# Order on TensorE between layers: where the transposes of normed token tiles stand among the products

## The chip, the cores and the metric

The kernel runs on one core of a Trainium2 chip, in one launch. The metric is device time in microseconds. Before the change it is 3289.97 us (median of 3 runs, 3287.52 to 3290.29).

## What is computed

One sequence of 1024 tokens of width 1024 (float32) goes through two blocks of layers. Cut to what matters here, the reference is:

```
x = layernorm(a * x + rglru_mla(x))          # layer A: gated linear recurrence beside causal attention
x = layernorm(a * x + ssd(x))                # SSD layer: chunked state space scan
x = x + 0.5 * rms(swiglu(rms(x, pre1)), post1)   # first feed-forward layer, 2816 hidden
x = x + rms(mix(rms(x, pre_mix)), post_mix)      # mix layer: dilated attention beside an S5 scan
x = x + 0.5 * rms(swiglu(rms(x, pre2)), post2)   # second feed-forward layer
```

Each layer ends with a product of [1024 tokens x its width] by its output weights, a residual add and norms over each token's 1024 channels. The next layer begins with products that contract over the channels.

## The kernel before

**Layout.** Inside a layer the activations are feature-major (channels on partitions, tokens in the free dimension). A layer's last product is made by token tile: 8 tiles of 128 tokens. `out_tile` (L695) makes one tile, 128 tokens x 1024 channels, as two halves of 512 columns. Every operand of a product is split in a high and a low part (`split`, L140 on ScalarE and L141 on VectorE or POOL), and each product is three products of these. Layer A's and the SSD layer's out tiles take 36 matmuls, those of the feed-forward and the mix layer 24.

**A layer's end.** For each token tile i: products (TensorE), add to the residual (VectorE: L1123 in the SSD layer), norm (VectorE statistics, ScalarE, VectorE or POOL for gain and bias, L675 to L681; then ScalarE squares L1138 and the scaling L1148 where the next layer has a norm of its own), a store, and then TensorE transposes that make the tile feature-major: 8 of 128x128 in `transpose_tokens` (L212, for the SSD layer and the mix layer), or 16 for a pair of tiles in `Ops.build` (L1194, for the feed-forward layers, whose products are made by a seven-product scheme on blocks, so that ScalarE, VectorE and POOL also form sums of the transposed blocks before they split them). Build j takes tiles 2j and 2j + 1.

**The next layer's start.** `lead` (L202) makes the first two products of the SSD and the mix layer, each in a half for tokens 0 to 511 (tiles 0 to 3) and one for 512 to 1023 (tiles 4 to 7): first both first halves, then both second ones, 24 matmuls each. In `ffn`, the first slice of the hidden layer is made by `hidden(0, 256)` and `hidden(256, 512)` (L1287), 84 matmuls of 256 columns each (each build fills 128 of 512 columns: the first half needs builds 0 and 1, the second builds 2 and 3); later slices take 512 columns at once.

**What sets the order.** The program is traced instruction by instruction, and then a list scheduler sets the order within each engine by its own estimate. `issue_after(i)` holds what is traced in it behind instruction i in that order (no wait, only the order). `anchor(K)` (L99) is the TensorE instruction traced last, and `turn` (L168) traces something behind it. Before the change, out tiles and transposes aren't held: the scheduler puts them where it finds room, and out tiles 0 and 1 fill gaps in the last attention head. `K.last` is the last out tile's last instruction, behind which the next layer's first products stand.

**Buffers.** Out tiles use two PSUM buffers (psA), transposes four (psB). The normed tiles of a pair lie in one buffer of a pool of four (P2); in the SSD layer's end weights hold two of these, so that tiles 4 and 5 can only be loaded when build 0 has read tiles 0 and 1.

Of the kernel before, what the change touches and what calls it, by code (L numbers as in the profile page):

```python
# [18 lines left out]
P = 128  # L19
# [3 lines left out]
NK = D // P  # L23
# [27 lines left out]
def _pools(ctx, tc):  # L51
    K = Ctx()
# [20 lines left out]
    K.n = 0  # L73
    K.last = None

# [117 lines left out]
def lead(K, ws, xt):  # L193


    out = [K.A() for _ in ws]
    with K.tc.issue_after(anchor(K) if K.last is None else K.last):
        for h in (0, 512):
            for a, w in zip(out, ws):
                for k in range(NK):  # L200
                    for m, (l, r) in enumerate(((w[0], "h"), (w[0], "l"), (w[1], "h"))):
                        K.nc.tensor.matmul(a[:, h:h + 512], l[:, k, :], xt(r, k)[:, h:h + 512],  # L202
                                           start=k == 0 and m == 0, stop=k == NK - 1 and m == 2)
    return out
# [547 lines left out]
def layer_a_out(K, I, ydram, zd, x1, XT):  # L752
# [4 lines left out]
    an = [K.heads[-1]] * 2  # L757
# [4 lines left out]
    for i in range(NT):  # L762
        with deferred(K, an[i]):
            if i % 2 == 0:
                yl = K.L(F32R)
            yv = stream_rows(K, ydram, 2, i, yl[:, 512 * (i % 2):512 * (i % 2) + 512], n=2)
            yv += stream_rows(K, ydram, 4, i, tail=K.tail)
            z2 = K.P2()
            z, zl = z2[:, 0, :], z2[:, 1, :]
            nc.sync.dma_start(zl, zd[i * P:(i + 1) * P, :])  # L770
        a = K.A()
        out_tile(K, a, w, lambda k: yv[k], 6)
        an.append(anchor(K))
        nc.vector.tensor_tensor(z, zl, a, ALU.add)
        layernorm(K, z, g, b)
        nc.sync.dma_start(x1[i * P:(i + 1) * P, :], z)
        transpose_tokens(K, z, i, XT)
    K.last = an[-1]

# [263 lines left out]
class SsdOut:  # L1043
# [53 lines left out]
    def rest(self, flip):  # L1097
# [14 lines left out]
        for i in range(NT):  # L1112
# [4 lines left out]
            with deferred(K, an[i]):  # L1117
                yv = dict(zip((10, 11), stream_rows(K, self.yd, 10, i, self.half(i), n=2)))
                yv.update(zip(range(12, 16), stream_rows(K, self.yd, 12, i)))
                nc.sync.dma_start(z, self.zd[i * P:(i + 1) * P, :])  # L1120
            out_tile(K, a, [w[k] for k in order], lambda k: yv[order[k]], 6, 3, flip if i == 0 else None)
            an.append(anchor(K))
# [4 lines left out]
            if i % 2:  # L1127
                ops.build(zt[:, 0, :], z, i // 2)
            K.m.append(marks(K))
        K.last = an[-1]  # L1130
        K.m = K.m[3::4]
# [93 lines left out]
def ffn(K, w_in, w_out, ops, xin, gain, post_g, done, extra=None):  # L1225
# [84 lines left out]
    for t in range(N_HID):  # L1310
        with behind(K, K.m[t]) if t < 2 else nullcontext():
            w = weights(t)
        pt = K.P2()
        if t == 0:
            with K.tc.issue_after(anchor(K) if K.last is None else K.last):
                hidden(w, pt, 0, 256)
                an = anchor(K)
                hidden(w, pt, 256, 512)
        else:
            hidden(w, pt, 0, 512)  # L1320
        nc.sync.dma_start(hd[t], pt[:, 0, :])
        tick(3)
# [125 lines left out]
    for i in range(NT):  # L1448
# [4 lines left out]
        o = (i % 2) * 512 + (i // 2) * P  # L1453
        out_tile(K, a, w, lambda k: (hid[k][:, 0, o:o + P], hid[k][:, 1, o:o + P]), 4)
        an.append(anchor(K))
        K.last = an[-1]
        y = acc[i // 2][:, i % 2, :]
# [330 lines left out]
def mix_out(K, I, ydram, zd, x3, x4, ops):  # L1788
# [8 lines left out]
    for i in range(NT):  # L1797
# [10 lines left out]
        a = K.A()  # L1808
        out_tile(K, a, w, lambda k: yv[k], 4)
        an.append(anchor(K))  # L1810
        nc.vector.tensor_tensor(z, z, a, ALU.add)
        post_norm(K, z, x, post, 1.0, junk, i < 6)
        nc.sync.dma_start(x4[tk, :], x)
        pre_norm(K, x, z)
        if i % 2:
            ops.build(zt[:, 0, :], z, i // 2)
        K.m.append(marks(K))
    K.last = an[-1]
    K.m = K.m[3::4]
# [105 lines left out]
def tile_two_blocks(ctx, tc, I, out):  # L1925
# [16 lines left out]
    def done(i, x, y):  # L1942
        nc.sync.dma_start(x3[i * P:(i + 1) * P, :], x)
        pre_norm(K, x, y)
        transpose_tokens(K, y, i, XT)

# [34 lines left out]
```

## Time and profile before

| | |
|---|---|
| time, median of 3 runs | 3289.97 us (3287.52 to 3290.29) |
| profiled execution | 3289.96 us, span 3288.2 us |
| mean granted clock of TensorE | 0.969 |
| TensorE busy | 3082.6 us (94%) |
| VectorE, ScalarE, POOL busy | 2210.6, 1625.5, 779.2 us (67%, 49%, 24%) |
| DMA | 398.97 MB, 121 GB/s on average |

The busy time of TensorE is the sum over its matmuls as the profile has them; the rest of the span it stands still. The clock is a share of full speed. The layer ends lie at about 400 to 545 us (layer A), 1290 to 1414 us (SSD layer), 2060 to 2140 us (first feed-forward layer) and 2500 to 2640 us (mix layer) of the span.

### The profile page before, as it was taken

The numbers are of one execution on the slowest core, as the hardware profiler recorded it, in microseconds if no ns is written. First come the engines' busy times: TensorE is split into PE (matmuls) and PEld (weight loads), VectorE is DVE, ScalarE is ACT, GpSimd is POOL, SyncE is SP. The second block draws the span as 40 slices with busy tenths as digits, with TensorE's granted clock in tenths as the row PEclk, the third lists the DMA queues.
The fourth block names the chain that finished last, engine by engine and source line by source line (L and its number), as shares of the span: only waits on it lengthen the run. The fifth ranks groups of instructions, "written<-read, shape, count | busy, mean of one in ns | idle before, by whom it ended". The sixth has DMA issues, their size and how long they took to land. (4 is left out here: it accounts for less than half of the span.)

```text
span 3288.2 us, 42188 instructions
## 1 busy us (share of the span) xinstructions
PE 3082.6 (94%) x15560; PEld 2572.9 (78%) x15560; DVE 2210.6 (67%) x3637; ACT 1625.5 (49%) x2945; POOL 779.2 (24%) x487
## 2 busy tenths in 40 slices
PE   8999899999999899689999899899999799999898
PEld 6887777888898778578778777688787688888777
DVE  6537777365748555887775789636666955455997
ACT  5526544355545522655555443642565755554442
POOL 0000001123322221622233434100000432332543
PEclk9999999999999999899999999999999899999999
DMA  4157442335344555323332620354564322224223
GB/s 129 55 181 234 121 132 87 87 82 125 87 116 97 173 162 162 99 97 116 103 126 81 224 83 30 131 178 175 151 165 139 136 84 90 77 84 150 107 84 116
DMA packets 349566, 398.97 MB, mean 121 GB/s; under 512 B 21168, under 2 KB 279344, under 8 KB 349360
## 3 DMA queue, kind: packets, MB, share of 16 engines
q1 hardware_dynamic: 324016, 379.50, 36.7%
q10 hardware_dynamic: 25344, 16.78, 1.6%
q8 instruction: 123, 2.02, 0.3%
q14 instruction: 83, 0.68, 0.1%
HBM read 279.29 MB, written 116.92 MB: 120 GB/s over the span
## 5 line engine op out<-in xcount | busy, mean ns | idle before, releaser
L141 DVE TENSOR_TENSOR wlo<-wst,whi 128x1024 fp32r<-128x1024 f32 (+1 forms) x190 | 234.1, 1235 | 355.2 <-ACT whi L140 337.2
L185 PE MATMUL pa<-x,whi 128*128 128x512 f32 x1568 | 428.6, 394 | 1.8 <-DVE l L141 0.9
L140 ACT ACTIVATE whi<-wst 128x1024 fp32r<-128x1024 f32 (+1 forms) x190 | 179.9, 948 | 350.9 <-PE pa L185 85.7
L147 ACT ACTIVATE wst<-wst,pk 128x128 f32<-128x128 f32 (+1 forms) x816 | 251.7, 391 | 181.8 <-DMA wst<-in_ffn_w_in_dram 116.0
L185 PEld LDWEIGHTS pa<-x,whi 128*128 128x128 f32 x1568 | 291.5, 188 | 63.9 <-DVE x L141 1.7
L185 PE MATMUL pa<-x,wlo 128*128 128x512 f32 x784 | 244.0, 392 | 2.0 <-DVE wlo L141 2.0
L1287 PE MATMUL pb<-x,whi 128*128 128x512 f32 (+1 forms) x736 | 224.2, 381 | 0.3 <-DVE r L141 0.3
L1287 PE MATMUL pa<-x,whi 128*128 128x512 f32 (+1 forms) x736 | 220.5, 382 | 1.0 <-DVE lnt L280 0.5
L1366 PE MATMUL pa<-wlo,whi 128*128 128x512 f32 x768 | 191.1, 407 | 16.7 <-DVE wlo L141 15.1
L1366 PEld LDWEIGHTS pa<-wlo,whi 128*128 128x128 f32 x768 | 151.0, 198 | 54.4 <-DVE wlo L141 19.9
L1366 PE MATMUL pb<-wlo,whi 128*128 128x512 f32 x744 | 178.8, 398 | 14.4 <-DVE wlo L141 14.4
L1250 POOL TENSOR_TENSOR s<-wst 128x512 f32<-128x512 f32 x44 | 57.7, 1311 | 562.1 <-ACT wst L147 524.3
L1366 PEld LDWEIGHTS pb<-wlo,whi 128*128 128x128 f32 x744 | 141.9, 192 | 47.3 <-DVE wlo L141 17.7
L185 PEld LDWEIGHTS pa<-x,wlo 128*128 128x128 f32 x784 | 147.2, 188 | 36.1 <-DVE wlo L141 4.5
L937 POOL TENSOR_TENSOR s<-s,p 128x1024 f32<-128x1024 f32 x32 | 64.5, 2016 | 448.1 <-DMA s<-d 337.5
L1287 PEld LDWEIGHTS pa<-x,whi 128*128 128x128 f32 x736 | 135.8, 189 | 28.5 <-ACT p L1290 1.6
L1287 PEld LDWEIGHTS pb<-x,whi 128*128 128x128 f32 x736 | 136.1, 188 | 26.9 <-DVE r L141 0.5
L140 ACT ACTIVATE whi<-s 128x1024 fp32r<-128x1024 f32 x88 | 93.0, 1057 | 112.6 <-POOL s L1251 59.9
L891 PE MATMUL pa<-whi,x 128*128 128x256 f32 x512 | 147.9, 289 | 0.0
L892 PE MATMUL pa<-wlo,x 128*128 128x256 f32 x512 | 145.0, 283 | 1.9 <-DVE wlo L141 1.9
L893 PE MATMUL pa<-whi,x 128*128 128x256 f32 x512 | 144.9, 283 | 0.0
L681 POOL TENSOR_TENSOR p<-p,q 128x1024 f32<-128x1024 f32 x8 | 21.1, 2643 | 513.7 <-DVE p L680 476.8
(580 smaller groups left out, 8067.8 us busy)
## 6 DMA issues: line engine op xcount, KB each, us to landing
wst<-in_ffn_w_in_dram SPq DMA_DIRECT2D x88, 512.0 KB, 3.8
d<-p SPq DMA_DIRECT2D x82, 512.0 KB, 3.5
d<-l SPq DMA_DIRECT2D x67, 512.0 KB, 3.9
x<-d SPq DMA_DIRECT2D x128, 256.0 KB, 5.4
p<-d SPq DMA_DIRECT2D x46, 512.0 KB, 4.6
wst<-in_s_w_in_dram SPq DMA_DIRECT2D x40, 512.0 KB, 4.1
s<-d SPq DMA_DIRECT2D x32, 512.0 KB, 9.5
l<-d SPq DMA_DIRECT2D x24, 512.0 KB, 6.0
```

The source lines that it names most:

```text
L140: K.nc.scalar.activation(hi, src, AF.Copy)
L141: (eng or K.nc.vector).tensor_tensor(lo, src, hi.bitcast(F32), ALU.subtract)
L147: K.nc.scalar.activation(st[:, k, :], st[:, k, :], AF.Copy, scale=col(K, gain, k0 + k))
L185: K.nc.tensor.matmul(ps[:, h:h + 512], w, x[:, h:h + 512], start=k == 0 and m == 0, stop=k == n - 1 and m == 2)
L681: nc.gpsimd.tensor_tensor(z, z, b, ALU.add)
L891: nc.tensor.matmul(o, xh, wh, start=k == 0, stop=False)
L892: nc.tensor.matmul(o, xh, wl, start=False, stop=False)
L893: nc.tensor.matmul(o, xl, wh, start=False, stop=k == NK - 1)
L937: nc.gpsimd.tensor_tensor(mv, mv, per_head(csT, P), ALU.subtract)
L1250: G(s1, a21, a22, ALU.add)
L1287: nc.tensor.matmul(p, l[:, k, :], r[:, k, :], start=k + m == 0, stop=k == 3 and m == 2)
L1366: nc.tensor.matmul(bank[j], th[:, a + o:a + o + P], tw[:, b:b + 512], start=c + m == 0, stop=c == n - 1 and m == 2)
```

## The change

All out tiles are now traced in `turn`, so that they run one after the other as traced. The transposes are no longer traced where their tile is normed: they are put on a list, `K.late`, and traced later, each behind the TensorE instruction traced last.

- Layer A: tile i - 2's transposes behind tile i's products; tiles 6 and 7 within `lead`, tile 6 behind the first product's first half, tile 7 behind the second's.
- SSD layer: build j in the middle (behind 18 of 36 matmuls) of out tile 2j + 3; build 3, of tiles 6 and 7, directly behind out tile 7, before any product of the feed-forward layer.
- First feed-forward layer: tile i - 3 behind tile i; tile 5 behind the first product's first half in `lead`, tiles 6 and 7 ahead of the second halves.
- Mix layer: build j behind out tile 2j + 3; build 3 between `hidden(0, 256)` and `hidden(256, 512)`.

The number of matmuls and of all other instructions is the same.

```
 def lead(K, ws, xt):
     out = [K.A() for _ in ws]
-    with K.tc.issue_after(anchor(K) if K.last is None else K.last):
-        for h in (0, 512):
-            for a, w in zip(out, ws):
-                ...
+    late, K.late = K.late, []
+    def product(a, w, h):
+        ...
+    keep = 3 if len(late) > 2 else 2
+    for h in (0, 512):
+        for a, w in zip(out, ws):
+            while late and (h or len(late) > keep):
+                turn(K, late.pop(0))
+            turn(K, lambda: product(a, w, h))
+            keep -= 1

 layer_a_out, per tile i
-        out_tile(K, a, w, lambda k: yv[k], 6)
+        turn(K, lambda: out_tile(K, a, w, lambda k: yv[k], 6))
         ...
-        transpose_tokens(K, z, i, XT)
-    K.last = an[-1]
+        K.late.append(lambda z=z, i=i: transpose_tokens(K, z, i, XT))
+        if i > 1:
+            turn(K, K.late.pop(0))
+    K.last = anchor(K)

 SsdOut.rest, per tile i
-            out_tile(K, a, [w[k] for k in order], lambda k: yv[order[k]], 6, 3, flip if i == 0 else None)
+            mid = flip if i == 0 else K.late.pop(0) if i > 2 and i % 2 else None
+            turn(K, lambda: out_tile(K, a, [w[k] for k in order], lambda k: yv[order[k]], 6, 3, mid))
             ...
             if i % 2:
-                ops.build(zt[:, 0, :], z, i // 2)
+                K.late.append(lambda zt=zt, i=i: ops.build(zt[:, 0, :], zt[:, 1, :], i // 2))
+            if i == 7:
+                turn(K, K.late.pop(0))
-        K.last = an[-1]
+        K.last = anchor(K)

 ffn, first slice
-            with K.tc.issue_after(anchor(K) if K.last is None else K.last):
+            with K.tc.issue_after(K.last):
                 hidden(w, pt, 0, 256)
                 an = anchor(K)
-                hidden(w, pt, 256, 512)
+                while K.late:
+                    turn(K, K.late.pop(0))
+                turn(K, lambda: hidden(w, pt, 256, 512))

 ffn, per out tile
-        out_tile(K, a, w, lambda k: (hid[k][:, 0, o:o + P], hid[k][:, 1, o:o + P]), 4)
+        turn(K, lambda: out_tile(K, a, w, lambda k: (hid[k][:, 0, o:o + P], hid[k][:, 1, o:o + P]), 4))
         an.append(anchor(K))
-        K.last = an[-1]
+        if len(K.late) > 2:
+            turn(K, K.late.pop(0))
 (its caller's done: transpose_tokens goes on K.late)

 mix_out, per tile i
-        out_tile(K, a, w, lambda k: yv[k], 4)
+        turn(K, lambda: out_tile(K, a, w, lambda k: yv[k], 4))
         an.append(anchor(K))
+        if i > 2 and i % 2:
+            turn(K, K.late.pop(0))
         ...
-            ops.build(zt[:, 0, :], z, i // 2)
+            K.late.append(lambda zt=zt, i=i: ops.build(zt[:, 0, :], zt[:, 1, :], i // 2))
```

**What moves on TensorE, SSD layer's end, builds 0 and 1.** Line numbers grow by 8 to 13 (L695 becomes L703, L1194 L1207, L1287 L1300). Here pa_10501 is out tile 5 before and pa_10260 is out tile 3 after; the transposes of p_10232 are build 1's, those of p_10023 build 0's. A name's number tells buffers apart. Before, in tile 5:

```order
L695 MATMUL pa_10501<-wlo_10014,s_10505 128x512 x2
L1194 MATMUL pb_10385<-ident,p_10232 128x128 [waits PE_49,Activation_49]
L1194 MATMUL pb_10385<-ident,p_10232 128x128 x3
L1194 MATMUL pb_10390<-ident,p_10232 128x128 [waits DVE_49]
L1194 MATMUL pb_10390<-ident,p_10232 128x128 x3
L695 MATMUL pa_10501<-whi_10013,s_10505 128x512 x2
L1194 MATMUL pb_10395<-ident,p_10232 128x128 [waits PE_49,Activation_49]
```

After, in tile 3:

```order
L703 MATMUL pa_10260<-p_9996,s_10264 128x512
L1207 MATMUL pb_10297<-ident,p_10023 128x128 [waits Activation_49]
L1207 MATMUL pb_10297<-ident,p_10023 128x128 x3
L1207 MATMUL pb_10302<-ident,p_10023 128x128 x4
L1207 MATMUL pb_10307<-ident,p_10023 128x128 [waits Activation_49]
L1207 MATMUL pb_10307<-ident,p_10023 128x128 x3
L1207 MATMUL pb_10312<-ident,p_10023 128x128 x4
L703 MATMUL pa_10260<-p_10001,s_10264 128x512 x6
```

Before, tile 2's and 3's transposes stood apart, near the end of tile 5 (and tile 0's and 1's in tiles 3 and 4); after, the 16 of a pair stand together in the middle of an out tile, tile 0's and 1's in tile 3 and tile 2's and 3's in tile 5.

**The same layer's end, TensorE's order at the start of the feed-forward layer.** pa_10866 is a product of `hidden(0, 256)`, p_10424 and p_10616 are the normed tiles of builds 2 and 3 before. Before:

```order
L1287 MATMUL pa_10866<-q_10189,whi_10835 128x256
L1287 MATMUL pa_10866<-q_10190,whi_10835 128x256
L1287 MATMUL pa_10866<-q_10189,wlo_10836 128x256
L1194 MATMUL pb_10577<-ident,p_10424 128x128 [waits Activation_49]
L1194 MATMUL pb_10577<-ident,p_10424 128x128 x3
L1194 MATMUL pb_10582<-ident,p_10424 128x128 x4
L1194 MATMUL pb_10587<-ident,p_10424 128x128 [waits Activation_49]
L1194 MATMUL pb_10587<-ident,p_10424 128x128 x3
L1194 MATMUL pb_10592<-ident,p_10424 128x128 x4
L1194 MATMUL pb_10769<-ident,p_10616 128x128 [waits PE_49,Activation_49]
```

After (pa_10654 is out tile 7, p_10577 holds tiles 6 and 7, pa_10852 is the first product of `hidden(0, 256)`):

```order
L703 MATMUL pa_10654<-wlo_10014,s_10658 128x512 x2
L703 MATMUL pa_10654<-whi_10013,s_10658 128x512 x2
L1207 MATMUL pb_10769<-ident,p_10577 128x128 [waits PE_49,Activation_49]
L1207 MATMUL pb_10769<-ident,p_10577 128x128 x3
L1207 MATMUL pb_10774<-ident,p_10577 128x128 [waits DVE_49]
L1207 MATMUL pb_10774<-ident,p_10577 128x128 x3
L1207 MATMUL pb_10779<-ident,p_10577 128x128 [waits PE_49,Activation_49]
L1207 MATMUL pb_10779<-ident,p_10577 128x128 x3
L1207 MATMUL pb_10784<-ident,p_10577 128x128 [waits DVE_49]
L1207 MATMUL pb_10784<-ident,p_10577 128x128 x3
L1300 MATMUL pa_10852<-r_10291,whi_10835 128x256
```

Before, 36 matmuls of `hidden(0, 256)` stood between out tile 7 and the transposes of builds 2 and 3; after, build 3 stands directly behind out tile 7 and all 168 matmuls of the first slice behind build 3 (build 2 is in the middle of tile 7).

**TensorE at the end of layer A's attention.** pb_3346 is the last head's product, pa_3472 out tile 0, pa_3556 out tile 1. Before:

```order
L695 MATMUL pa_3472<-r_3450,s_3464 128x512
L695 MATMUL pa_3556<-r_3450,s_3548 128x512 x2
L400 MATMUL pb_3346<-p_1625,q_1510 128x256 [waits Activation_49]
L695 MATMUL pa_3472<-r_3450,s_3464 128x512 [waits DVE_49]
L695 MATMUL pa_3472<-r_3450,s_3464 128x512 x3
L695 MATMUL pa_3556<-r_3450,s_3548 128x512 x4
L400 MATMUL pb_3346<-p_1625,q_1510 128x256 [waits DVE_49]
```

After:

```order
L703 MATMUL pa_3472<-r_3450,s_3464 128x512
L408 MATMUL pb_3346<-p_1625,q_1510 128x256 [waits Activation_49]
L703 MATMUL pa_3472<-r_3450,s_3464 128x512 [waits DVE_49]
L703 MATMUL pa_3472<-r_3450,s_3464 128x512 x3
L408 MATMUL pb_3346<-p_1625,q_1510 128x256 [waits DVE_49]
```

Before, matmuls of out tiles 0 and 1 stood among the last heads' products, 30 of them tile 1's; after, only out tile 0's do, and all 36 of tile 1 stand behind tile 0's last.

## Rows read from the trace of the kernel before

**Rows 1.** The page, span and busy time of each engine.

```profile
span 3288.2 us, 42188 instructions
...
PE 3082.6 (94%) x15560; PEld 2572.9 (78%) x15560; DVE 2210.6 (67%) x3637; ACT 1625.5 (49%) x2945; POOL 779.2 (24%) x487
```

**Rows 2.** TensorE's waits, 1290 to 1400 us: total, times, longest.

```profile
PE pb L1194 <- ACT p L1148: 22.6, 5, 10.9
```

**Rows 3.** TensorE's timeline, 1294 to 1430 us: start, us, line, count, idle before.

```profile
1302.25 0.61 PE L695 MATMUL pa<-whi,l 128*128 128x512 f32 x2
...
1310.41 0.61 PE L695 MATMUL pa<-whi,l 128*128 128x512 f32 x2
...
1316.08 1.03 PE L1194 MATMUL pb<-ident,p 128*128 128x128 f32 x8
...
1345.54 1.97 PE L1194 MATMUL pb<-ident,p 128*128 128x128 f32 x8 [7.78 <-ACT p L1148]
1347.51 1.19 PE L695 MATMUL pa<-whi,l 128*128 128x512 f32 x2
...
1364.76 0.40 PE L1287 MATMUL pa<-r,whi 128*128 128x256 f32 x2
...
1384.72 1.97 PE L1194 MATMUL pb<-ident,p 128*128 128x128 f32 x8 [10.89 <-ACT p L1148]
...
1395.34 1.97 PE L1194 MATMUL pb<-ident,p 128*128 128x128 f32 x8 [2.54 <-ACT p L1148]
...
1413.52 0.70 PE L1287 MATMUL pa<-r,whi 128*128 128x512 f32 x2 [0.25 <-DVE p L1296]
```

**Rows 4.** ScalarE's timeline there: last activation of tiles 0, 1 and 7.

```profile
1313.55 1.15 ACT L1148 ACTIVATE p<-p,pns 128x1024 f32<-128x1024 f32 x1 [0.74 <-DVE pns L280]
...
1322.07 1.16 ACT L1148 ACTIVATE p<-p,pns 128x1024 f32<-128x1024 f32 x1
...
1394.14 1.15 ACT L1148 ACTIVATE p<-p,pns 128x1024 f32<-128x1024 f32 x1 [0.64 <-ACT x L140]
```

**Rows 5.** VectorE's timeline there: add of tiles 0 and 1.

```profile
1297.80 1.22 DVE L1123 TENSOR_TENSOR p<-p,pa 128x1024 f32<-128x1024 f32 x1
...
1303.43 1.22 DVE L1123 TENSOR_TENSOR p<-p,pa 128x1024 f32<-128x1024 f32 x1
```

**Rows 6.** POOL's timeline there: splits of build 0.

```profile
1334.58 2.54 POOL L141 TENSOR_TENSOR x<-p,x 128x512 fp32r<-128x512 f32 x2
...
1341.23 1.26 POOL L141 TENSOR_TENSOR q<-p,q 128x512 fp32r<-128x512 f32 x1
```

**Rows 7.** Windows: length, busy of PE, PEld, DVE, ACT, POOL, PEclk, DMA.

```profile
1340.00:1350.00 10.00, 4.46 (x15) 3.62 (x16) 7.26 (x15) 3.66 (x7) 2.49 (x2) 0.66 0.53 184
...
1380.00:1390.00 10.00, 3.94 (x16) 3.13 (x16) 8.16 (x28) 8.78 (x18) 2.35 (x1) 0.50 0.48 152
...
1400.00:1410.00 10.00, 10.00 (x84) 10.00 (x84) 7.12 (x16) 7.98 (x23) 1.27 (x2) 0.98 0.01 2
```

**Rows 8.** SP's queue there: loads of tiles 4 to 7.

```profile
1342.52 15.00 SPq L1120 DMA_DIRECT2D p<-d  x4
```

**Rows 9.** TensorE's waits, layer A's end (390 to 545 us).

```profile
PE pb L212 <- POOL p L681: 4.1, 1, 4.1
PE pa L695 <- ACT s L140: 3.8, 2, 3.2
```

**Rows 10.** Windows at the three other ends, columns as in rows 7.

```profile
530.00:540.00 10.00, 5.88 (x28) 4.41 (x27) 4.67 (x6) 3.40 (x5) 3.24 (x2) 0.84 0.26 107
...
2120.00:2130.00 10.00, 7.28 (x24) 5.90 (x25) 2.92 (x6) 6.79 (x15) 0.00 (x0) 0.53 0.00 0
...
2590.00:2600.00 10.00, 1.12 (x4) 0.72 (x4) 10.00 (x22) 10.00 (x27) 8.53 (x5) 0.58 0.31 127
```

**Rows 11.** TensorE's waits, first feed-forward layer's end (2060 to 2150 us).

```profile
PE pb L212 <- ACT p L1148: 8.0, 3, 5.1
```

**Rows 12.** TensorE's waits, mix layer's end (2540 to 2640 us).

```profile
PE pa L1287 <- ACT whi L140: 7.6, 1, 7.6
```

More of the change, by code (lines that the diff above doesn't have):

```diff
@@ L73, in _pools @@
     K.n = 0
-    K.last = None
+    K.last, K.late = None, []
     def nm(p):
@@ L196, in lead @@
     out = [K.A() for _ in ws]
-    with K.tc.issue_after(anchor(K) if K.last is None else K.last):
-        for h in (0, 512):
-            for a, w in zip(out, ws):
[L200 to L203, printed above, removed]
+    late, K.late = K.late, []
+    def product(a, w, h):
+        for k in range(NK):
+            for m, (l, r) in enumerate(((w[0], "h"), (w[0], "l"), (w[1], "h"))):
+                K.nc.tensor.matmul(a[:, h:h + 512], l[:, k, :], xt(r, k)[:, h:h + 512],
+                                   start=k == 0 and m == 0, stop=k == NK - 1 and m == 2)
+    keep = 3 if len(late) > 2 else 2
[5 more added lines that the diff above has]
+            keep -= 1
     return out
@@ L1815, in mix_out @@
         if i % 2:
-            ops.build(zt[:, 0, :], z, i // 2)
+            K.late.append(lambda zt=zt, i=i: ops.build(zt[:, 0, :], zt[:, 1, :], i // 2))
         K.m.append(marks(K))
-    K.last = an[-1]
+    K.last = anchor(K)
     K.m = K.m[3::4]
@@ L1944, in done @@
         pre_norm(K, x, y)
-        transpose_tokens(K, y, i, XT)
+        K.late.append(lambda: transpose_tokens(K, y, i, XT))
     ffn(K, I["ffn1_w_in"], I["ffn1_w_out"], ops, x2, "ffn1", I["ffn1_post_g"], done, s5_prep(K, I))
```

## The prediction

> **What bounds the kernel now.** The page comes first: its span, and TensorE's busy time. TensorE works 3082.6 of 3288.2 us [rows 1], so all that a new order can win is the 205 us in which it stands still, and whatever it makes TensorE wait is paid in full. The profiled execution took 3289.96 us, 1.8 us more than its span and 0.01 us from the median of the three runs, so the sum below is made against 3289.96. About 0.2%, 6.6 us, is what a measurement of this kernel can tell from no change.
>
> The change touches four places, where one layer's last eight token tiles are multiplied out, normed, transposed on TensorE and split for the next layer. I read the list of TensorE's waits there, then its timeline, then the other engines' at the same place. At the end of the SSD layer TensorE waits 22.6 us for the second norm's last activation, L1148 [rows 2]. The timeline shows where [rows 3]: transposes of tile 0 stand between products without a wait (1316.08, eight in 1.03 us), those of tile 3 come after 7.78 us of idleness (1345.54), those of tiles 4 to 7 start after 10.89 us more (1384.72) and end with tile 7's at 1395.34. Between the last out tile and that wait, 36 of the 84 products of the feed-forward layer's first half slice run (from 1364.76).
>
> **The SSD layer's end, the largest term.** The new order on TensorE is: tile 3's first 18 products, the 16 transposes of tiles 0 and 1, its other 18; the same in tile 5 for tiles 2 and 3, in tile 7 for tiles 4 and 5; then the transposes of tiles 6 and 7, and behind them all 168 products of the first slice. Nothing on TensorE may pass a transpose that waits. Removed is nothing, added nothing: all products and transposes stay, so the price is the idle time.
>
> A tile's 36 products take 8.16 us (1302.25 to 1310.41 [rows 3]), 0.227 us each. Between the end of tile 1 and the transposes that need it lie tile 2 and half of tile 3, 54 x 0.227 = 12.2 us. How long does a tile take from its last product to being normed? Tile 1's products end at 1302.25 and its last activation ends at 1322.07 + 1.16 = 1323.23 [rows 3, 4], 21.0 us. Tile 0 took 1313.55 + 1.15 - 1297.80 = 16.9 us from its add on VectorE [rows 4, 5], and the add of tile 1 came 1.2 us after its last product (1303.43 [rows 5]). 16.9 + 1.2 = 18.1: I take 18 us, with 16.9 (no lag at all) and 21.0 as ends. Tile 7 needed 1395.29 - 1364.76 = 30.5 us [rows 3, 4], with the next layer's weight work in the same queues; I don't take that, because its chain in the changed order has less in front of it, but it says on which side the error may lie. On POOL the new order puts each tile's norm behind the splits of the transposes just issued, and those are 1.3 us each [rows 6].
>
> 18 is more than 12.2, so each of the four groups of transposes waits. After such a wait the clock is at 1.2 GHz: 0.66 was granted over 1340 to 1350, 0.50 over 1380 to 1390 [rows 7], and eight transposes take 1.97 us, not 1.03 [rows 3]. So 16 take 3.9 us, and the 18 products behind them 4.1 + 1.2 = 5.3 us, since the first ones are still slow (two in 0.98 us at 1347.51 [rows 3], where two at 2.4 GHz take 0.45).
>
> By steps: the first group starts at 1323.2, tile 3 ends at 1323.2 + 3.9 + 5.3 = 1332.4; the second starts at 1332.4 + 18 = 1350.4, tile 5 ends at 1359.6, and tile 6 and half of tile 7 fit in the next 18 us. The third starts at 1377.6, tile 7 ends at 1386.8, and the fourth starts at 1404.8, with nothing of TensorE's beside the whole of tile 7's norm. At 1408.7 the first slice begins; its 168 products of 256 columns take 168 x 0.119 = 20.0 us (84 in 10 us over 1400 to 1410 [rows 7]). The second slice then starts near 1428.7, where before it started at 1413.5 [rows 3]: **+15 us**. In short the term is 3 x latency - 38.8. At 16.9 us it is +12, at 21.0 it is +24. Were TensorE at 2.4 GHz throughout (2.1 + 4.1 us a step in place of 9.2, 2.1 for the last group), it would lose another 11 us: at 16.9 us of latency that leaves **+1**. The ends are +1 and +24.
>
> The loads of tiles 4 to 7 wait on SP's queue for the first group's last split to free their buffer (four issues from 1342.52 [rows 8], just after POOL's split at 1341.23 [rows 6]). In the new order that group starts 7 us later than tile 0's transposes did, but all at once, so I let the loads come when they came; they are 5 us late at worst, within the ends. The waits give VectorE, ScalarE and POOL no more work. Who waits behind: hidden, and through it the whole first feed-forward layer.
>
> **Layer A's end.** TensorE waits 4.1 us for tile 7's transposes [rows 9], and the clock is slow around it (0.84 over 530 to 540, some 1.6 us [rows 10]). Before and after, 48 products of the SSD layer stand ahead of those transposes, so they gain only what tile 7's norm gains: the transposes of tiles 4 to 6 come sooner and their splits leave VectorE's queue ahead of it, 0 to 6 us. Given back: 30 products of out tile 1 filled the last attention head and now stand behind it, up to 30 x 0.227 = 6.8 us. But there was a wait of 3.2 us just there for a split (the larger part of 3.8 [rows 9]) which tile 1's products can now fill. I take 0, the ends are -6 and +7.
>
> The Trainium skill speaks against this part: "Perfetto Trace Analysis", section "Optimization Strategy", says that where the most contended engine changes over time, mixing the stages can help, and the change takes such mixing out. By that rule all 6.8 us would be lost and the sum would be 3309; the rows, with a wait beside it that the same products fill, leave it near 0.
>
> **First feed-forward layer's end.** Waits of 8.0 us for tiles 4, 6 and 7 [rows 11], the clock at 0.53 after them [rows 10]. The transposes of tile 5 move ahead of the second first-half product, by 5 us. Their splits leave ScalarE sooner, so tile 7's norm, queued behind them, can end some 2 us sooner: **-2**. At best it is 6 us (the wait of 5.1 in there, and some clock), at worst +4: tile 5 isn't normed where it is asked for, and 24 products stand behind it.
>
> **Mix layer's end.** VectorE is busy 10.00 of 10 us and TensorE 1.12 over 2590 to 2600 [rows 10], with 7.6 us of waiting for a weight split [rows 12]. The order of TensorE can't shorten VectorE's work; the last transposes now come after 84 products instead of among them. **-1**, from -6 (most of that wait) to +6 (the same again, for tile 7).
>
> **Sum**: 0 + 15 - 2 - 1 = +12, so 3289.96 + 12 = **3302 us**.
>
> **Rivals.**
> 1. Norms finish early. While TensorE waits, the others have less to do, and the latency is at the low end with little slow clock: +1 at the SSD layer, sum +1 - 3 = -2, 3288 us. For it: tile 0's 16.9 us [rows 4, 5]. Against it: POOL's splits in front [rows 6] and tile 7's 30.5 us. 0.18.
> 2. Faster. The transposes issued early take their splits out of ScalarE's and VectorE's queues before the last tile's norm, which then ends 5 us sooner at layer A's and the first feed-forward layer's end: -6 there, -6 there, and +2 at the SSD layer: -10, 3280 us. It decides if the latency at the SSD layer is below about 15 us (3 x 15 - 38.8 = +6, less the slow clock). For it: the waits of 4.1 and 8.0 us [rows 9, 11]. Against it: no tile in the trace was normed that soon. 0.14.
> 3. Mixing is lost (the page's rule above, as a mechanism of this kernel): the last head has only out tile 0 to fill with, and layer A costs +6.8: 3309 us. Against it: the wait of 3.2 us [rows 9]. 0.10.
> 4. The change does nothing that counts: the order was as good as this already at three places, and the waits at the fourth come out alike: 3290 us. Against it: the 36 products that stood before the last waits now stand behind them. 0.05.
>
> **How the numbers follow.** My forecast has 0.53 of the chance. Below 3283.4 lies rival 2 with a hair of rival 1: 0.15. Within 6.6 us of 3290 lie rivals 1 and 4 (0.18 + 0.05, less that hair): 0.22. The rest, the forecast and rival 3, is slower: 0.63. The forecast's own band is 3296 to 3314 (the SSD layer's term at +12 to +24, the others near their values). The range reaches down over rivals 1 and 4 and stops above rival 2, whose 0.14 it leaves out with the forecast's tail: 3284 to 3314.
>
> **What would show it.** Right: at the SSD layer's end four waits of transposes for L1148's counterpart in the new file, the last one the longest (some 15 us, before the feed-forward layer's first product), each followed by a clock near 0.5; the second slice starting 10 to 20 us later against the end of tile 1; the three other ends within 6 us of before. Wrong: a latency under 15 us in those rows, a first product of the feed-forward layer that comes as early as before, or a layer A whose attention loses more than 5 us of TensorE's time.

## The result and the profile after

The changed kernel takes **3318.35 us** (median of 4 runs, 3317.75 to 3320.36), beside 3289.18 us for the kernel before on the same chip (4 runs, 3287.52 to 3290.29): 29.2 us (0.9%) more by the medians, a ratio of 1.0096 with an interval of 1.0083 to 1.0108. The forecast was slower by 12 us, at most by 24.

The page first, against [rows 1]:

```profile
span 3316.2 us, 42147 instructions
...
PE 3078.8 (93%) x15560; PEld 2572.7 (78%) x15560; DVE 2225.8 (67%) x3637; ACT 1627.1 (49%) x2945; POOL 754.7 (23%) x487
```

TensorE's work is the same to 4 us, so the 28.0 us of span are time in which it stands still. TensorE's waits at the SSD layer's end (1280 to 1450 us), against the 22.6 us of [rows 2]; L1207 and L1161 are the transposes of a build and the norm's last activation, L1194 and L1148 before:

```profile
PE pb L1207 <- ACT p L1161: 46.4, 5, 15.5
```

TensorE's timeline there, against [rows 3]: all transposes of a build, and at other places the row in which a tile's or a slice's products begin or end.

```profile
1313.86 1.03 PE L1207 MATMUL pb<-ident,p 128*128 128x128 f32 x8
1322.00 1.97 PE L1207 MATMUL pb<-ident,p 128*128 128x128 f32 x8 [7.11 <-ACT p L1161]
...
1329.85 0.62 PE L703 MATMUL pa<-whi,l 128*128 128x512 f32 x2
...
1342.10 1.03 PE L1207 MATMUL pb<-ident,p 128*128 128x128 f32 x8
1352.48 1.97 PE L1207 MATMUL pb<-ident,p 128*128 128x128 f32 x8 [9.36 <-ACT p L1161]
...
1358.86 0.62 PE L703 MATMUL pa<-whi,l 128*128 128x512 f32 x2
...
1371.10 1.03 PE L1207 MATMUL pb<-ident,p 128*128 128x128 f32 x8
1386.02 1.97 PE L1207 MATMUL pb<-ident,p 128*128 128x128 f32 x8 [13.88 <-ACT p L1161]
...
1392.22 0.61 PE L703 MATMUL pa<-whi,s 128*128 128x512 f32 x2
1393.43 1.10 PE L1207 MATMUL pb<-ident,p 128*128 128x128 f32 x8 [0.59 <-ACT p L1161]
1410.02 1.97 PE L1207 MATMUL pb<-ident,p 128*128 128x128 f32 x8 [15.49 <-ACT p L1161]
1411.63 0.78 PE L1300 MATMUL pa<-r,whi 128*128 128x256 f32 x2
...
1433.37 0.70 PE L1300 MATMUL pa<-r,whi 128*128 128x512 f32 x2 [0.61 <-DVE p L1309]
```

Four long waits, each for the odd tile of a pair, and the longest ahead of the feed-forward layer's first product (1411.63). The second slice starts at 1433.37, 19.9 us later than in [rows 3]. Tile 1 ends 0.6 us sooner here, so this place costs 20.5 us.

To find the other 7.5 us I take the same points of the program in both traces and compare the stages between them. The points are the last product of a `lead`, the end of the SSD layer's out tile 1, the first out tile of a feed-forward layer, the first 512-column product of a first slice, the start of the last 48 products ahead of the second feed-forward layer's out tiles, and the last matmul. Differences from the profiled execution of before, in us (from one profiled execution each; columns 1, 3, 5 and 6 hold the four ends that the prediction lists):

| kernel | layer A and its end | to the SSD out tiles | SSD end | first ffn's slices | its end | mix layer and its end | second ffn, up to its out tiles | to the last matmul |
|---|---|---|---|---|---|---|---|---|
| after | 0.3 | -0.9 | **20.5** | -3.1 | -2.7 | **6.8** | **2.7** | **4.3** |
| e1 | 0.2 | 3.4 | 16.1 | -2.1 | -3.2 | 2.7 | 0.0 | 0.0 |
| e2 | -4.9 | -3.0 | 1.9 | -2.4 | -2.1 | 7.4 | 3.8 | 4.7 |
| e3 | -4.3 | -0.7 | 20.6 | -3.7 | -3.7 | -2.6 | -0.7 | 6.9 |
| e4 | 1.6 | 0.2 | 21.7 | -2.3 | -4.4 | 7.3 | 3.2 | 0.8 |
| e5 | 0.6 | -0.4 | 18.1 | -1.2 | -3.7 | 5.4 | 2.0 | 6.5 |
| e6 | -2.8 | -0.7 | 20.1 | -3.5 | -4.5 | 9.2 | 1.9 | 5.2 |
| e7 | -4.0 | -1.7 | 6.0 | -1.7 | -1.9 | 1.2 | -2.1 | 0.8 |
| e8 | -4.6 | -2.7 | 2.2 | 0.2 | -2.1 | -0.5 | -0.9 | 0.8 |
| e9 | 0.9 | -0.5 | 22.4 | -2.2 | -5.4 | 12.0 | 3.8 | 4.5 |
| e10 | 0.3 | -1.8 | 18.0 | -1.7 | -2.4 | 6.9 | 1.1 | 6.7 |
| e11 | -2.3 | -1.0 | -0.5 | -1.6 | 1.5 | 2.7 | -1.1 | 5.1 |
| e12 | -0.9 | -1.5 | 26.9 | 1.3 | -0.8 | 5.3 | 5.4 | 0.0 |

The rows e1 to e12 are the experiments below. Stages whose code is as in before move by up to 4 us too (e7's layer A -4.0, e1's first ffn's end -3.2), so only the four bold numbers stand for something, and those by the rows that share them. Two were on no list of mine. TensorE's waits at layer A's end (390 to 560 us), against [rows 9]:

```profile
PE pa L703 <- ACT s L140: 5.0, 2, 3.2
PE pb L220 <- POOL p L689: 3.3, 1, 3.3
```

At the first feed-forward layer's end (2060 to 2200 us), against [rows 11]:

```profile
PE pb L220 <- ACT p L1161: 6.2, 3, 5.0
```

At the mix layer's end (2490 to 2700 us), against [rows 12]:

```profile
PE pb L1207 <- ACT p L1161: 14.7, 3, 11.4
PE pb L1207 <- DVE r L141: 6.1, 1, 6.1
...
PE pa L1300 <- ACT r L140: 3.7, 1, 3.7
```

And in the second feed-forward layer's out tiles (3050 to 3320 us), where before had none for L695, the same line:

```profile
PE pa L703 <- ACT whi L140: 2.0, 2, 1.7
...
PE pa L703 <- DVE wlo L141: 1.1, 2, 0.5
```

The first two ends wait as before to 2 us. At the mix layer's the wait for a weight split (7.6 us) is gone, and transposes wait instead.

The prediction's sum was 12 us, the stages above add up to 27.9. Of the 15.9 us between them 5.5 lie at the SSD layer's end, 7.8 at the mix layer's and 7.0 in the two stages that were on no list; the other stages take back 4.4.

### The profile page after: what moved, and what is told of

It reads as the page before. It is cut to its first block, busy times and chain, and to the rows that moved or that the text cites. A ratio compares the mean times of both kernels' runs of the same rounds, so it can differ in the third digit from the quotient of the medians.

```text
span 3316.2 us, 42147 instructions
## 1 busy us (share of the span) xinstructions
PE 3078.8 (93%) x15560; PEld 2572.7 (78%) x15560; DVE 2225.8 (67%) x3637; ACT 1627.1 (49%) x2945; POOL 754.7 (23%) x487
## 5 line engine op out<-in xcount | busy, mean ns | idle before, releaser
L1300 PE MATMUL pb<-x,whi 128*128 128x512 f32 (+1 forms) x736 | 224.6, 381 | 0.0
L1300 PE MATMUL pa<-x,whi 128*128 128x512 f32 (+1 forms) x736 | 220.2, 382 | 0.7 <-ACT p L1303 0.7
L1300 PEld LDWEIGHTS pa<-x,whi 128*128 128x128 f32 x736 | 136.6, 189 | 27.4 <-ACT p L1303 1.0
L1300 PEld LDWEIGHTS pb<-x,whi 128*128 128x128 f32 x736 | 135.9, 188 | 26.4 <-issue 0.4
L1300 PE MATMUL pa<-x,wlo 128*128 128x512 f32 (+1 forms) x368 | 140.0, 381 | 0.0
```

Of the source, the lines that this page charges most:

```text
L1300: nc.tensor.matmul(p, l[:, k, :], r[:, k, :], start=k + m == 0, stop=k == 3 and m == 2)
```

## The experiments

Each kernel was timed against the kernel before on its own chip. Times are medians with lowest and highest, ratios with their interval.

**e1: the SSD layer's end alone.** The kernel before, with only this changed:

```
-            out_tile(K, a, ..., flip if i == 0 else None)
+            mid = flip if i == 0 else K.late.pop(0) if i > 2 and i % 2 else None
+            turn(K, lambda: out_tile(K, a, ..., mid))
-                ops.build(zt[:, 0, :], z, i // 2)
+                K.late.append(lambda zt=zt, i=i: ops.build(...))
+            if i == 7:
+                turn(K, K.late.pop(0))
-        K.last = an[-1]
+        K.last = anchor(K)
```

> The kernel before, with the SSD layer's end alone in the new order. Theory (each end pays for itself): the second slice of the first feed-forward layer starts 21 us later as in the changed kernel, 4 us of which the same layer's later stages give back, so 3290 + 17 to 21 = 3307 to 3311 us. Rival (the loss comes from the ends together, each moving what the next finds): under 3300 us.

**e2: all but that end.** The changed kernel with these lines as before.

> The changed kernel, with the SSD layer's end as before. Theory: 3318 less 17 to 21 = 3297 to 3301 us, and the second slice starts within 2 us of where it did before. Rival (the ends aren't independent): 3305 us or more.

**e3: all but the mix layer's end.**

```
-        turn(K, lambda: out_tile(K, a, w, lambda k: yv[k], 4))
+        out_tile(K, a, w, lambda k: yv[k], 4)
-        if i > 2 and i % 2:
-            turn(K, K.late.pop(0))
-            K.late.append(lambda zt=zt, i=i: ops.build(...))
+            ops.build(zt[:, 0, :], z, i // 2)
```

> The changed kernel, with the mix layer's end as before. Theory (the mix layer's end costs 7 us, since out tiles 0 and 1 no longer start VectorE's chain during the last attention head): 3318 - 7 = 3311 us. Rival (that end costs nothing by itself, it only comes after a different attention): 3318 us.

**e4: the second feed-forward layer's out tiles free**, the one place where out tiles are held though nothing follows them.

```
-        turn(K, lambda: out_tile(K, a, w, ..., 4))
+        with K.tc.issue_after(anchor(K)) if gain == "ffn1" else nullcontext():
+            out_tile(K, a, w, ..., 4)
```

> The changed kernel, with the out tiles of the second feed-forward layer free to be placed among other products, as before. There are no transposes behind them. Theory (holding them one behind the other costs 5 to 9 us): 3318 - 5 to 9 = 3309 to 3313 us. Rival (what is lost there came with the shifted stages before it): 3318 us.

Measured: e1 3304.33 us (3298.05 to 3307.38), ratio 1.0049 (1.0034 to 1.0064). e2 3299.45 (3295.44 to 3305.17), 1.0038 (1.0023 to 1.0053). e3 3304.56 (3299.73 to 3307.89), 1.0053 (1.0036 to 1.0070). e4 3314.20 (3310.76 to 3318.28), 1.0082 (1.0067 to 1.0097).

So of the 29.2 us, each kernel against the one before on its own chip (3287.73 us for these four), undoing the SSD layer's end gives back 17.5, the mix layer's 12.4 and the last out tiles 2.7. e1 lies 16.6 us above it. The interval of e4 overlaps that of the changed kernel, so its time alone doesn't show a gain; the place does. By place 20.5 falls to 1.9 in e2; 6.8 and 2.7 fall to -2.6 and -0.7 in e3; 4.3 falls to 0.8 in e4. For the last one TensorE's timeline of the changed kernel shows why:

```profile
3259.98 0.73 PE L703 MATMUL pa<-whi,q 128*128 128x512 f32 x2 [0.33 <-ACT whi L140]
3261.24 0.74 PE L703 MATMUL pa<-wlo,q 128*128 128x512 f32 x2 [0.53 <-DVE wlo L141]
...
3264.13 0.73 PE L703 MATMUL pa<-whi,q 128*128 128x512 f32 x2 [1.67 <-ACT whi L140]
```

Tile 0 uses each weight row as it is split, and nothing else may run in the gaps: in the first 10 us of these out tiles (3256.8 to 3266.8) TensorE is busy for 6.94 us. In the kernel before, products of several tiles stand between each other there, and the first 10 us of its out tiles (3232.9 to 3242.9) are full (10.00).

**e8: the new order only at layer A's and the first feed-forward layer's end** (the edits of e2, e3 and e4 together).

> The changed kernel with the SSD layer's end, the mix layer's end and the second feed-forward layer's out tiles as before: the new order is left at layer A's end and at the first feed-forward layer's end. Theory (the loss lies at the three places undone; these two are worth 0 to -4 us): 3284 to 3289 us. Rival (layer A loses the filling of its last head): 3292 us or more.

Measured: 3285.60 us (3280.26 to 3289.40, 11 runs), 0.9990 (0.9981 to 0.9999). At these two ends the order costs nothing; if it gains, it is within what can be told from no change.

**e5: build 3 between the halves of the first slice**, as in the mix layer: the two lines `if i == 7: turn(K, K.late.pop(0))` of the SSD layer's end are left out.

> The changed kernel, with the transposes of tiles 6 and 7 of the SSD layer's end between the two halves of the first slice, and no longer ahead of it. Theory (the last wait of 15.5 us is there because nothing of TensorE's lies beside tile 7's norm): the 84 products of the first half cover 10 us of it, the second slice starts 10 us sooner, 3318 - 10 = 3308 us. Rival (the norm's end is set by VectorE, ScalarE and POOL, whose work for the first slice then runs into it): tile 7 is normed later by as much, 3314 us or more.

Measured: 3310.82 us (3310.51 to 3317.23), 1.0071 (1.0057 to 1.0085); at the place itself 18.1 us, 2.4 less. TensorE's timeline of this kernel:

```profile
1411.57 1.97 PE L1205 MATMUL pb<-ident,p 128*128 128x128 f32 x8 [6.30 <-ACT p L1159]
1418.07 0.58 PE L1298 MATMUL pa<-r,whi 128*128 128x256 f32 x1 [4.53 <-ACT r L140]
```

The last wait falls from 15.49 to 6.30 us, since the first half slice now runs beside tile 7's norm. But the splits of 16 transposes at once come out behind them (4.53 us), with a granted clock of 0.50 over 1410 to 1420 us, so in this trace most of it is paid again. The profiled execution was the slowest of e5's four (3317.23 us): by the medians, each against its own before, e5 gains 6.1 us, between the theory's 10 and the rival's 4 or less, and where the rest of the gain lies this trace doesn't show.

**e10: weight work later.** In the SSD layer's end, a table of marks places the next layer's first weight work in the queues (at tiles 3 and 7): `K.m = K.m[3::4]` becomes `K.m = [K.m[6], K.m[7]]`.

> The changed kernel, with the work on the first slice's weights (ScalarE, VectorE, POOL) queued behind tile 6's norm at the SSD layer's end, where it was queued behind tile 3's. Theory (tile 5 is normed 27 us after its products and not 18 because this work stands ahead of it in the engines' queues): the third wait of 13.9 us falls to about 9, the last one grows by at most 2, and the second slice starts 3 us sooner, 3315 us. Rival (build 1's splits and tile 4's norm make tile 5 late): the third wait stays within 2 us of 13.9, and the weights make the first slice wait, 3318 us or more.

Measured: 3317.72 us (3316.80 to 3319.76), 1.0096 (1.0081 to 1.0112). TensorE's timeline:

```profile
1376.56 1.97 PE L1207 MATMUL pb<-ident,p 128*128 128x128 f32 x8 [4.99 <-ACT p L1161]
1386.53 1.91 PE L1207 MATMUL pb<-ident,p 128*128 128x128 f32 x8 [3.23 <-ACT p L1161]
1406.19 1.97 PE L1207 MATMUL pb<-ident,p 128*128 128x128 f32 x8 [17.76 <-ACT p L1161]
```

The third wait falls from 13.88 to 4.99 us: that work did make tile 5 late. It has to be done ahead of the feed-forward layer all the same, now in front of tiles 6 and 7, which wait 3.23 and 17.76 us. The place gains 2.5 us, the kernel nothing.

**e7: the SSD layer's end, each build one out tile later.** The kernel before with e1's edit, but builds 0 and 1 in the middle of tiles 4 and 6 and the other two between the halves of the first slice:

```
-            mid = flip if i == 0 else K.late.pop(0) if i > 2 and i % 2 else None
+            mid = flip if i == 0 else K.late.pop(0) if i in (4, 6) else None
-            if i == 7:
-                turn(K, K.late.pop(0))
```

> The kernel before, with the SSD layer's end alone in a new order, and each build one tile later than in the change: build 0 in the middle of out tile 4, build 1 in that of out tile 6, builds 2 and 3 between the two halves of the first slice. 54 products of cover become 90, 20.4 us, and 12.2 + 10 us lie ahead of the last two. Theory (what counts is cover against a latency of 18 to 27 us): the first two waits go, the last is some 12 us, the second slice starts 10 to 16 us sooner than before the change, 3274 to 3280 us. Rival (late builds hold the buffers of tiles 4 to 7, whose loads then hold up the norms): what is won in the first waits comes back in front of tile 7, and the time is 3288 us or more.

Measured: 3286.99 us (3284.64 to 3292.61, 11 runs), 0.9998 (0.9989 to 1.0007). TensorE's timeline, then SP's queue and VectorE's timeline:

```profile
1316.97 2.08 PE L1195 MATMUL pb<-ident,p 128*128 128x128 f32 x16
...
1340.45 1.19 PE L695 MATMUL pa<-whi,l 128*128 128x512 f32 x2 [9.13 <-DVE p L1124]
1346.49 1.91 PE L1195 MATMUL pb<-ident,p 128*128 128x128 f32 x16
```

```profile
1335.50 0.81 SPq L1120 DMA_DIRECT2D p<-d  x2
```

```profile
1339.09 1.22 DVE L1124 TENSOR_TENSOR p<-p,pa 128x1024 f32<-128x1024 f32 x1 [1.85 <-DMA p<-d]
```

With one more tile ahead of them the transposes find their tiles normed and wait no more: a tile and a half of cover was too little, two and a half is enough. A wait of 9.13 us stands in another place. Tile 4's residual is loaded only at 1335.50, when build 0's splits have freed the buffer; its add comes at 1339.09, and the product that needs the add's PSUM buffer waits for it. That is the rival's mechanism. It isn't all: behind out tile 7 the first slice's products and the last two builds wait 21.5 us in pieces of up to 4.9, for weight splits, norms and splits of transposed blocks, where TensorE waited 17.7 us before. In its trace this end keeps 6.0 us of loss, and the kernel is where it was before, not 10 to 16 us faster.

**e6: the mix layer's out tiles 0 to 2 free.** The idea was that they lost their place in the gaps of the last attention head.

```
-        turn(K, lambda: out_tile(K, a, w, lambda k: yv[k], 4))
+        with K.tc.issue_after(anchor(K)) if i > 2 else nullcontext():
+            out_tile(K, a, w, lambda k: yv[k], 4)
```

> The changed kernel, with out tiles 0 to 2 of the mix layer free to stand among the last attention head's products, as before; the builds stay late. Theory (the mix layer's end is late because VectorE's chain starts late, with out tile 0): VectorE is again over 9 of 10 us busy during the last head, the second slice of the second feed-forward layer starts some 7 us sooner against the end of the first one, 3311 us. Rival (the builds' places make it late): no change, 3318 us.

Measured: 3316.94 us (3315.24 to 3321.52), 1.0087 (1.0074 to 1.0101); the mix layer at +9.2, no better than the +6.8 with all held. The idea fell. TensorE's timeline shows where the early tiles are given back, at builds 0 and 2:

```profile
2572.45 3.68 PE L1207 MATMUL pb<-ident,p 128*128 128x128 f32 x16 [8.28 <-ACT p L1161]
...
2617.61 3.75 PE L1207 MATMUL pb<-ident,p 128*128 128x128 f32 x16 [15.30 <-ACT p L1161]
...
2639.35 0.58 PE L1300 MATMUL pa<-r,whi 128*128 128x256 f32 x1 [5.60 <-ACT r L140]
```

**e9: the mix layer's builds later.** `if i > 2 and i % 2` becomes `if i > 4 and i % 2`: builds 0 and 1 behind tiles 5 and 7, the others between the halves.

> The changed kernel, with the mix layer's builds 0 and 1 two tiles later: build 0 behind out tile 5, build 1 behind out tile 7, builds 2 and 3 between the halves of the first slice. Theory (transposes that wait hold up the out tiles behind them, so VectorE, which bounds this end, gets their sums late): VectorE's adds of tiles 4 to 7 come at least 8 us sooner against those of tile 0, and the second slice of the second feed-forward layer starts 6 to 9 us sooner against the end of the first one: 3318 - 7 = 3311 us. Rival (holding out tiles one behind the other is what costs): no change there, 3318 us.

Measured: 3323.63 us (3317.23 to 3327.00), 1.0108 (1.0091 to 1.0125); the mix layer at +12.0. The adds of tiles 4 to 7 did come 1 to 10 us sooner, but tile 7 was normed 7.7 us later, and the splits of two builds stand exposed. TensorE's waits from 2490 to 2700 us:

```profile
PE pa L1300 <- ACT r L140: 9.1, 2, 4.6
PE pa L1300 <- DVE ro L281: 5.8, 1, 5.8
```

What cured the SSD layer's waits makes this end worse.

**e11: only the tiles in a row.** The kernel before, with each layer's out tiles one after another and the transposes free, as they were:

```
-        out_tile(K, a, w, ...)
+        with K.tc.issue_after(an[-1] if i else anchor(K)):
+            out_tile(K, a, w, ...)
```

> The kernel before, with half of the change: all out tiles one behind the other, the transposes free as before. Theory (the held transposes make the SSD layer's and the mix layer's end late, the held out tiles the second feed-forward layer's): the second slices of both feed-forward layers start within 4 us of before, measured from the layer ahead of each, the last out tiles end 4 to 5 us later, 3292 us. Rival (holding the out tiles costs at the mix layer too, by later adds): 3300 us or more.

**e12: only the transposes held.** The changed kernel with each `turn(K, lambda: out_tile(...))` as the bare call again.

> The changed kernel, with the other half alone: the transposes held late, the out tiles free. Theory: the SSD layer's end +16 to 20 us, the mix layer's +7 to 9, the second feed-forward layer's out tiles 0 to 1: 3309 to 3314 us. Rival (a waiting transpose costs only because out tiles may not pass it): out tiles go ahead of it, both ends come within 5 us of before, 3295 us or less.

Measured: e11 3294.48 us (3286.44 to 3297.57, 10 runs), 1.0020 (1.0011 to 1.0029), with nothing at the SSD layer's end and +5.1 at the last out tiles. e12 3322.24 us (3320.23 to 3326.15), 1.0104 (1.0087 to 1.0121), 8 us above its theory, with nothing at the last out tiles, +5.3 at the mix layer and +26.9 at the SSD layer's end. Its waits there (1280 to 1450 us):

```profile
PE pb L1207 <- ACT p L1161: 40.9, 4, 15.0
PE pa L703 <- ACT x L140: 5.2, 1, 5.2
```

Freedom for the out tiles doesn't help. Some do go ahead: in TensorE's timeline 31 and 36 products stand between the transposes of the two tiles of builds 0 and 1, and their waits shrink to nothing and 4.46 us. But build 2 waits 10.07 and 11.28 us for its two tiles, build 3 15.04. So the loss at the layers' ends comes from the held transposes, and of the held tiles only the last ones show a cost beyond what unedited stages move by.

## Why the prediction was right in its sign and too small

**The SSD layer's end, +15 predicted, +20.5 measured.** The mechanism stands: the order puts each pair's norm in series with the products. e1 has the loss with this end alone, e2 has it gone with this end alone undone, and e7 shows that more cover removes the waits for the transposes. The prediction's own steps against the trace (a tile ends where the next one's first pair starts, tile 7 0.45 us after its last pair starts):

| step | predicted | measured |
|---|---|---|
| tile 1's half of the first group starts | 1323.2 | 1322.00 |
| tile 3 ends | 1332.4 | 1329.85 |
| tile 3's transposes start | 1350.4 | 1352.48 |
| tile 5 ends | 1359.6 | 1358.86 |
| tile 5's transposes start | 1377.6 | 1386.02 |
| tile 7 ends | 1386.8 | 1392.67 |
| tile 7's transposes start | 1404.8 | 1410.02 |
| second slice starts | 1428.7 | 1433.37 |

The step that failed is "I take 18 us". From the end of its products to its norm, tile 1 took 20.3 us, tile 3 22.6, tile 5 27.1 and tile 7 17.3: the three that I took as 54 are 67.0, 13 us more, of which 9.1 are tile 5's alone. ScalarE's timeline shows tile 3 (normed by the L1161 at 1351.28), tile 5 (1384.82) and, between them, what stands in one queue with them:

```profile
1343.12 0.63 ACT L1151 ACTIVATE j<-p 128x512 bf16<-128x512 f32 x1 [1.47 <-POOL p L689]
...
1345.79 1.24 ACT L687 ACTIVATE p<-p,lnt 128x1024 f32<-128x1024 f32 x1 [1.94 <-DVE lnt L686]
1346.93 0.61 ACT L1151 ACTIVATE j<-p 128x512 bf16<-128x512 f32 x1
...
1351.28 1.15 ACT L1161 ACTIVATE p<-p,pns 128x1024 f32<-128x1024 f32 x1 [3.65 <-issue]
1352.34 4.78 ACT L147 ACTIVATE wst<-wst,pk 128x128 f32<-128x128 f32 x16
...
1369.46 1.05 ACT L140 ACTIVATE whi<-wst 128x1024 fp32r<-128x1024 f32 x1
...
1372.60 1.24 ACT L687 ACTIVATE p<-p,lnt 128x1024 f32<-128x1024 f32 x1 [1.14 <-DVE lnt L686]
...
1384.82 1.15 ACT L1161 ACTIVATE p<-p,pns 128x1024 f32<-128x1024 f32 x1 [1.04 <-DVE pns L288]
```

Tile 3's second square (1346.93) stands behind tile 4's L687, which waits for tile 4's statistics, so a norm that TensorE waits for is held up by one that it does not. Tile 5 finds build 1's splits and the next layer's weight work (1352.34, 1369.46) in front of it. I had read the latency from tile 0 and tile 1, which stood ahead of all builds, and set aside tile 7's 30.5 us of before [rows 3, 4]. Even these two took more than 18: tile 1's 21.0 us I kept as an end only, and tile 0's 16.9 run from its add, which came 3.7 us after its products had ended (at 1294.09), so it took 20.6. e10 shows that the weight work makes 8.9 us of tile 5's wait. (One count was wrong too: in the trace of before 48 products of the first slice, not 36, stand between out tile 7 and the last two builds. The sum doesn't use it.)

The other error went the other way and took back 6.7 us. I let all 16 transposes of a group and the 18 products behind them wait and run slowly, 9.2 us a step; measured are 7.85, 6.38 and 6.65. (The first group's earlier start and the last steps give 1.7 us more: 15.2 + 13.0 - 6.7 - 1.7, and the 0.6 us by which tile 1 was early, are the 20.4.) The even tile's eight transposes did not wait but ran in 1.03 us; only the odd tile's took 1.97. The windows of the changed kernel show the clock, with the columns of [rows 7]:

```profile
1320.00:1330.00 10.00, 8.00 (x27) 6.71 (x28) 5.80 (x16) 7.40 (x15) 7.20 (x4) 0.60 0.15 55
...
1400.00:1410.00 10.00, 0.00 (x0) 0.00 (x0) 3.22 (x11) 3.83 (x6) 2.34 (x1) 0.50 0.39 112
```

**The mix layer's end, -1 predicted, +6.8 measured**, just outside its band of -6 to +6. The step that failed is "the last transposes now come after 84 products instead of among them": the sum gives it nothing, the range a wait for tile 7, and the builds ahead of the last one have no term at all. Tile 7 costs no wait: it is normed at 2633.78 us, and build 3 follows the first 84 products at 2636.72 without one. What TensorE waits for is tile 5. Build 2, of tiles 4 and 5, now stands ahead of all 84 products, and they stand still with it for 11.44 us. TensorE's timeline of the kernel before, for tile 5's transposes:

```profile
2602.22 1.97 PE L1194 MATMUL pb<-ident,p 128*128 128x128 f32 x8 [0.25 <-ACT p L1148]
```

And of the changed kernel, for tile 5's, all of build 3's, and the first product behind these; last, ScalarE's timeline for tile 7's norm:

```profile
2623.46 1.97 PE L1207 MATMUL pb<-ident,p 128*128 128x128 f32 x8 [11.44 <-ACT p L1161]
...
2636.72 1.91 PE L1207 MATMUL pb<-ident,p 128*128 128x128 f32 x16
2642.30 1.31 PE L1300 MATMUL pa<-r,whi 128*128 128x256 f32 x2 [3.68 <-ACT r L140]
```

```profile
2632.63 1.15 ACT L1161 ACTIVATE p<-l,pns 128x1024 f32<-128x1024 f32 x1 [1.54 <-DVE pns L288]
```

Against the end of `lead` tile 5's transposes start 7.1 us later than before, and from there to the second slice it takes 32.2 us where it took 32.6: the whole loss lies ahead of them. The wait of 10.9 to 11.9 us for tile 5 stands in all of the kernels with this order at the mix layer (e2, e4, e5, e10). Ahead of it build 1 waits 6.1 us for a split, with out tiles 6 and 7 behind it, whose adds on VectorE come 10.7 and 12.8 us later than before. What makes tile 5's norm late stays open: earlier sums, with the 84 products ahead of build 2 (e9), do not help, and neither do early tiles (e6).

Sixteen transposes in one piece also leave their first split with nothing beside it, 3.68 us here; e6 and e9 have the same line at 5.60 and twice some 4.6, e5 at the SSD layer's end at 4.53. In e3, with this end undone, the same 16 stand in groups of four and eight among products. Since the 32.2 us are no more than before, that isn't where this end lost. In the table all kernels with these transposes held lie at +5.3 to +12.0, all others at -2.6 to +2.7.

**"The change touches four places."** It touches more. The second feed-forward layer's out tiles go through the same line as the first's and are held too: +4.3, and 4.5 to 6.9 in all kernels with that line but 0 to 0.8 in those without. And ahead of them, in a stretch where no line was edited (2634.8 to 3222.0 us of before), the list scheduler orders TensorE's, VectorE's and ScalarE's instructions differently where the mix layer's transposes are held: +1.1 to +5.4 us in every kernel that holds them, -2.1 to 0 in every other. That the two go together is shown; what in that order costs the time is not.

**Layer A's end, 0 predicted, +0.3 measured; the first feed-forward layer's, -2 predicted, -2.7 measured.** The first agrees, but a stage of this length moves by more than 5 us with the same code (last section), so one trace can't show it; e8's time shows that the two ends together cost nothing. The granted clock from 530 to 540 us is 1.00, where it was 0.84 [rows 10]; the wait there is 3.3 us for 4.1, now for tile 6. The second only looks right: e1 and e7, whose code there is that of before, show -3.2 and -1.9 too.

**The rivals.** The first (norms early) and the second (faster) fell with the latency: no odd tile of the changed kernel was normed in under 17.3 us. The fourth (nothing that counts) fell at the first result. The third put the loss of mixed stages at layer A, and there it fell: out tile 1's 30 products cost nothing that the runs show. The Trainium skill's rule, "Perfetto Trace Analysis", section "Optimization Strategy", that mixing stages with different limits can help, is not borne out by layer A, and no other place here tests it. The last out tiles lost a filling of another kind (4.3 us by place, 0.8 in e4): there gaps between weight rows were filled with other tiles' products of the same stage, and the change took that out. I had asked what fills the gaps at one place and not at each place where the edited helper is called.

## What to carry to other kernels

A written order on an in-order engine puts the other engines' latencies in series with it. It pays only where the work put between is longer than that latency, and the latency has to be read from a tile in the middle of the queues, with the splits and weight work of its neighbours in front of it (27.1 us here), from the end of its products and not from its add on VectorE (16.9 for the first tile). A piece of transposes placed ahead of a run of products makes these wait for its last tile (11.44 us at the mix layer). Transposes gathered into one piece also gather what follows them, so that their first split has no cover. And a helper that is edited is edited for all its callers: list them, the last layer too, and expect a scheduler to move unedited work as well.

## What was not expected of the chip

Transposes are no slow work in themselves: at the SSD layer's end of the changed kernel eight of 128x128 fp32 took 1.03 us between products, three times, and 1.97 us behind a wait, four times, at the same line. And time moves by itself: in the changed kernel and eight of the others (e2 to e6, e8 to e10) the traces show the same instructions in the same order on every engine up to the end of layer A's stage, and that stage lay between -4.9 and +1.6 us of before, so a gain of 2 us at one end can't be read from one trace.
